# A decoder trunk with product-key experts: VectorE makes the low halves of all V blocks

## The chip, the core and the metric

The kernel runs on one core of a Trainium2 chip. The metric is the device time of one execution in microseconds, from three runs of the kernel before. TensorE does the matmuls, VectorE, ScalarE and GpSimd the elementwise work, and SyncE (SP) issues all the transfers. In profiles they are called PE (PEld for its weight loads), DVE, ACT, POOL and SP.

## What is computed

Two decoder layers on 256 tokens of width 1024. Each layer mixes the tokens (a state-space part and two kinds of attention) and then adds a retrieval of experts. The change concerns the last one, which is cut here to its core:

```python
def peer_ffn(h, wq, k1, k2, u, v):   # u, v: 16384 x 1024
    q = (xc @ wq).reshape(PEER_CHUNK, PEER_HEADS, 2, PEER_HALF)
    ...
    # per token and head: 16 experts e and gates g = softmax(sc)
    u_sel = u[e]
    v_sel = v[e]
    pre = jnp.einsum("td,thkd->thk", xc, u_sel)
    act = jax.nn.gelu(pre, approximate=False) * g
    return jnp.einsum("thk,thkd->td", act, v_sel)
```

Beside this, each layer scales, shifts and gates its inputs by rows that come from a conditioning vector: `mod = silu(c) @ ada_w[l] + ada_b[l]`.

## The kernel before

The kernel gathers nothing: it computes every expert for every token and gives most of them a gate of zero. The 16384 experts are 128 blocks of 128. In the **U stage** each block of `uT` is multiplied with the 256 normed tokens, and a GELU follows; the gates are multiplied in. In the **V stage** each block's activations (128 experts by 256 tokens) are multiplied with the block of `vT` (128 experts by 1024 columns), and all 128 blocks are summed in four PSUM banks, `pacc` (two halves of the tokens by two halves of the columns).

All matmuls are to be near fp32 precision. So every operand is split into a high half, its rounding to fp32r, and a low half, the rest, and a product is made of three matmuls (`mm3`, lines 166 to 168): high by high, high by low, low by high. For a block of V the steps are these:

- `fetch` (L145 to 149): SP issues one transfer of 512 KB into `raw`, a ring of five buffers.
- `split` (L151 to 163): ScalarE rounds it to the high half `wH` (L159); VectorE or GpSimd subtracts for the low half `wL` (L162). Both have rings of three buffers. The argument `low` chooses the engine: "v" is VectorE, anything else GpSimd.
- `v_parts` (L875 to 887): ScalarE rounds the activations to `aH` (L879), VectorE makes `aL` (L880), then comes `split`.
- twelve matmuls of 512 columns: two by two banks, three products each.

The engine of the low half of V block n is set at line 892: GpSimd for n = 0, 3, 6 and so on, 43 of 128 blocks, VectorE for the other 85. In the U stage line 847 and the default of line 684 choose it. They stay.

In layer 0 the V stage carries more: 56 **modulation steps** (`ada_ahead`, L186 to 205) that compute the conditioning rows of the layer's last gate and of layer 1. A step is a transfer of 512 KB into `adaw` (L196), a ring of four, and on VectorE a product with the conditioning row that sums along the way (L178); every second step also adds the bias to two columns (L181). `spread` (L855) hands them out over the blocks in the order in which the code is written.

The order of the instructions on each engine is fixed when the kernel is built. A scheduler walks the program with its own estimate of each duration and issues what it takes to be ready, so VectorE's modulation steps and the transfers on SP are drawn ahead of where `spread` puts them when it holds VectorE to be free. On the chip every engine works through its list in order. Also drawn ahead into layer 0's V stage is GpSimd's work for the masks of layer 1's attention (L335 to 344), and the row of gates that TensorE spreads over the partitions (`gate_row`, L277) and the conditioning row itself (`cond_row`, L127).

```python
        low = lambda n: "g" if n % 3 == 0 else "v"
        for n in range(NKEY - LAST):
            mm = v_parts(n, low(n))
            for c in range(NC):
                for h in range(2):
                    mm(c, h)
            spread(pend, min(1.0, (n + 1) / (NKEY - 8)), len(todo))
```

Of the kernel before, what the change touches and what calls it, by code (L numbers as in the profile page):

```python
# [82 lines left out]
def trunk(ctx: ExitStack, tc: tile.TileContext, x_in, c_in, ada, cols, rows, w_in, w_out, wq, keysT, uT, vT, fg, out, dbg=None):  # L83
# [589 lines left out]
    def peer(l, steps):  # L673
# [215 lines left out]
        h_pool[0].close()  # L889
        todo = steps(es.enter_context(tc.tile_pool(name=f"cond{l}", bufs=1, reuse_waits="tile", side="right")))  # L890
        pend = list(enumerate(todo))
        low = lambda n: "g" if n % 3 == 0 else "v"
        for n in range(NKEY - LAST):
            mm = v_parts(n, low(n))
            for c in range(NC):
# [21 lines left out]
    for l in range(DEPTH):  # L917
# [20 lines left out]
        def steps(pool):  # L938
# [6 lines left out]
            return ada_ahead(jobs, pool)  # L945

        acc = peer(l, steps)
        xs = ExitStack()
        xp = xs.enter_context(tc.tile_pool(name=f"x{l + 1}", bufs=1, reuse_waits="tile"))
# [90 lines left out]
```

## Time and profile before

| | |
|---|---|
| median of three runs | 1995.51 us (1990.01 to 1998.99) |
| the profiled execution: its own time | 1995.14 us |
| its span in the trace | 1993.4 us |
| TensorE matmuls, busy | 1883.4 us (94%) |
| VectorE, busy | 1440.0 us (72%) |
| ScalarE, busy | 966.0 us (48%) |
| GpSimd, busy | 776.0 us (39%) |
| moved by transfers | 376.50 MB, 189 GB/s on average |

Busy shares are averages over stages of different kinds. Matmuls are pipelined: one begins before the one ahead of it has ended, so the pace is read from the starts. The same holds for short VectorE instructions, whose durations overlap a little. An idle time in brackets stands before its instruction, with what ended it.

### The profile page before, as it was taken

The numbers are of one execution on the slowest core, as the hardware profiler recorded it, in microseconds if no ns is written. First come the engines' busy times: TensorE is split into PE (matmuls) and PEld (weight loads), VectorE is DVE, ScalarE is ACT, GpSimd is POOL, SyncE is SP. The second block draws the span as 40 slices with busy tenths as digits, with TensorE's granted clock in tenths as the row PEclk, the third lists the DMA queues.
The fourth block names the chain that finished last, engine by engine and source line by source line (L and its number), as shares of the span: only waits on it lengthen the run. The fifth ranks groups of instructions, "written<-read, shape, count | busy, mean of one in ns | idle before, by whom it ended". The sixth has DMA issues, their size and how long they took to land.

```text
span 1993.4 us, 33885 instructions
## 1 busy us (share of the span) xinstructions
PE 1883.4 (94%) x12864; PEld 1717.4 (86%) x12864; DVE 1440.0 (72%) x2746; ACT 966.0 (48%) x1502; POOL 776.0 (39%) x441
## 2 busy tenths in 40 slices
PE   4898998999999998999989989989999999999998
PEld 3787998999999786788877889979999998888886
DVE  6975999889963998855554669998899435555555
ACT  3564544454444444454545544445444444555444
POOL 5775787000024234322246657960000342222333
PEclk9898999999999999999989989989999999999999
DMA  8863554444455998855634334544444555665653
GB/s 285 281 208 124 164 181 165 134 162 155 160 168 177 348 350 311 295 196 193 194 121 138 127 130 149 189 150 155 155 160 159 177 181 190 206 215 192 195 194 116
DMA packets 103559, 376.50 MB, mean 189 GB/s; under 512 B 12002, under 2 KB 12258, under 8 KB 102756
## 3 DMA queue, kind: packets, MB, share of 16 engines
q1 hardware_dynamic: 103396, 374.34, 55.7%
q8 instruction: 100, 1.64, 0.3%
q14 instruction: 63, 0.52, 0.1%
HBM read 371.15 MB, written 3.15 MB: 188 GB/s over the span
## 4 chain that ended last, share of the span: by engine, by line
PE 69%; DVE 21%; POOL 3%; issue 2%; ACT 2%; DMA 2%; SPq 0%; POOLq 0%; ACTq 0%; DVEq 0%
PE pacc L167 11%; PE pacc L168 10%; PE pacc L166 10%; PE pu L166 9%; PE pu L168 9%; PE pu L167 9%; POOL wL L162 2%; PE pa L167 1%; DVE eq L765 1%; PE pa L168 1%; PE pa L166 1%; DVE eq L764 1%; DVE raw L178 1%; DVE fi L766 1%; DVE a L760 1%
## 5 line engine op out<-in xcount | busy, mean ns | idle before, releaser
L162 POOL TENSOR_TENSOR wL<-raw,wH 128x1024 fp32r<-128x1024 f32 (+2 forms) x364 | 719.8, 1992 | 1142.9 <-ACT wH L159 1134.3
L159 ACT CAST wH<-raw 128x1024 fp32r<-128x1024 f32 (+1 forms) x602 | 628.5, 1045 | 517.7 <-PE pu L167 345.2
L166 PE MATMUL pu<-hH,wH 128*128 128x256 f32 x2048 | 581.5, 284 | 4.8 <-ACT wH L159 2.8
L168 PE MATMUL pu<-hH,wL 128*128 128x256 f32 x2048 | 576.2, 281 | 3.8 <-POOL wL L162 3.8
L167 PE MATMUL pu<-hL,wH 128*128 128x256 f32 x2048 | 575.0, 281 | 0.0
L162 DVE TENSOR_TENSOR wL<-raw,wH 128x1024 fp32r<-128x1024 f32 x324 | 399.3, 1233 | 130.9 <-ACT wH L159 130.8
L167 PE MATMUL pacc<-wL,aH 128*128 128x512 f32 x1024 | 401.4, 392 | 11.6 <-POOL wL L162 8.7
L168 PE MATMUL pacc<-wH,aL 128*128 128x512 f32 x1024 | 399.3, 390 | 0.0
L166 PEld LDWEIGHTS pu<-hH,wH 128*128 128x128 f32 x2048 | 387.5, 189 | 5.3 <-ACT wH L159 3.0
L168 PEld LDWEIGHTS pu<-hH,wL 128*128 128x128 f32 x2048 | 388.0, 189 | 4.3 <-POOL wL L162 4.3
L167 PEld LDWEIGHTS pu<-hL,wH 128*128 128x128 f32 x2048 | 388.1, 189 | 0.0
L880 DVE TENSOR_TENSOR aL<-act,aH 128x256 fp32r<-128x256 f32 x256 | 164.1, 642 | 224.2 <-ACT aH L879 223.7
L166 PE MATMUL pacc<-wH,aH 128*128 128x512 f32 x1024 | 277.7, 389 | 1.2 <-ACT wH L159 1.2
L879 ACT CAST aH<-act 128x256 fp32r<-128x256 f32 x256 | 103.9, 407 | 357.0 <-PE pacc L167 354.7
L167 PEld LDWEIGHTS pacc<-wL,aH 128*128 128x128 f32 x1024 | 192.8, 188 | 57.4 <-POOL wL L162 11.7
L166 PEld LDWEIGHTS pacc<-wH,aH 128*128 128x128 f32 x1024 | 191.9, 188 | 41.4 <-ACT wH L159 1.6
L168 PEld LDWEIGHTS pacc<-wH,aL 128*128 128x128 f32 x1024 | 192.8, 188 | 39.6
L166 PE MATMUL pa<-hH,wH 128*128 128x256 f32 x256 | 75.4, 308 | 13.8 <-ACT hH L260 10.9
L167 PE MATMUL pa<-hL,wH 128*128 128x256 f32 x256 | 76.8, 303 | 1.8 <-DVE hL L261 1.8
L168 PE MATMUL pa<-hH,wL 128*128 128x256 f32 x256 | 76.3, 301 | 1.5 <-POOL wL L162 1.5
L178 DVE SCALAR_TENSOR_TENSOR adaw<-adaw,crow 128x1024 f32<-128x1024 f32 x56 | 70.0, 1259 | 1.2 <-ACT crow L130 1.2
L841 DVE SCALAR_TENSOR_TENSOR act<-pc,act 128x160 f32<-128x160 f32 (+30 forms) x126 | 38.4, 305 | 41.2 <-PE pc L835 40.7
(428 smaller groups left out, 2498.6 us busy)
## 6 DMA issues: line engine op xcount, KB each, us to landing
raw<-in_uT_dram SPq DMA_DIRECT2D x256, 512.0 KB, 3.5
raw<-in_vT_dram SPq DMA_DIRECT2D x256, 512.0 KB, 4.2
adaw<-in_ada_dram SPq DMA_DIRECT2D x56, 512.0 KB, 6.1
raw<-in_ada_dram SPq DMA_DIRECT2D x40, 512.0 KB, 4.5
raw<-in_w_in_dram SPq DMA_DIRECT2D x38, 512.0 KB, 4.1
raw<-in_wq_dram SPq DMA_DIRECT2D x32, 512.0 KB, 3.5
raw<-in_w_out_dram SPq DMA_DIRECT2D x16, 512.0 KB, 3.5
raw<-in_w_in_dram SPq DMA_DIRECT2D x8, 392.0 KB, 3.9
```

The lines of the kernel that those rows point to most:

```text
L159: A.copy(h[:, :n], src)
L162: eng.tensor_tensor(out=lo[:, o:o + step], in0=src[:, o:o + step], in1=h[:, o:o + step].bitcast(F32), op=ALU.subtract)
L166: T.matmul(o, l[0], r[0], start=start, stop=False)
L167: T.matmul(o, l[0], r[1], start=False, stop=False)
L168: T.matmul(o, l[1], r[0], start=False, stop=stop)
L178: V.scalar_tensor_tensor(out=src, in0=src, scalar=1.0, in1=cond, op0=ALU.mult, op1=ALU.mult, accum_out=modc[:, m, k:k + 1])
L760: V.scalar_tensor_tensor(out=a0, in0=a0, scalar=-8.0, in1=ci, op0=ALU.mult, op1=ALU.add)
L764: V.tensor_tensor(out=eq, in0=wide(fab)[:, :, :, None].to_broadcast([P, 2 * NC, TK, TK]), in1=iotar[:, None].to_broadcast([P, 2 * NC, TK, ...
L765: V.tensor_tensor(out=eq, in0=eq, in1=wide(fii)[:, :, None, :].to_broadcast([P, 2 * NC, TK, TK]), op=ALU.mult)
L841: V.scalar_tensor_tensor(out=a, in0=pv[:, lo:hi, :], scalar=1.0 / WSCALE, in1=a, op0=ALU.mult, op1=ALU.mult)
L879: A.copy(aH, act)
L880: V.tensor_tensor(out=aL, in0=act, in1=aH.bitcast(F32), op=ALU.subtract)
```

## The change

One line: the choice of the engine in the V stage no longer depends on the block.

```diff
         h_pool[0].close()
         todo = steps(es.enter_context(tc.tile_pool(name=f"cond{l}", bufs=1, reuse_waits="tile", side="right")))
         pend = list(enumerate(todo))
-        low = lambda n: "g" if n % 3 == 0 else "v"
+        low = lambda n: "v"
         for n in range(NKEY - LAST):
             mm = v_parts(n, low(n))
```

The scheduler places the rest anew. On GpSimd, from the end of layer 0's U stage to the first work of layer 1 (rows of 128x1024 are subtractions of the U and V stages, those of 128x512 belong to layer 1's projections), before:

```order
L162 TENSOR_TENSOR wL<-raw,wH 128x512 x32
L162 TENSOR_TENSOR wL<-raw,wH 128x1024 x51
L123 MEMSET ones 1x128
L162 TENSOR_TENSOR wL<-raw,wH 128x1024 x15
L335 MEMSET mle 128x128
L337 MEMSET mgt 128x128
...
L343 AFFINE_SELECT mask_s<-mask_s 128x128 x2
L344 AFFINE_SELECT mask_s<-mask_s 128x128
L162 TENSOR_TENSOR wL<-raw,wH 128x1024 x30
L162 TENSOR_TENSOR wL<-raw,wH 128x512 x2
```

and of the change:

```order
L162 TENSOR_TENSOR wL<-raw,wH 128x512 x32
L162 TENSOR_TENSOR wL<-raw,wH 128x1024 x51
L123 MEMSET ones 1x128
L162 TENSOR_TENSOR wL<-raw,wH 128x1024 x2
L335 MEMSET mle 128x128
L337 MEMSET mgt 128x128
...
L343 AFFINE_SELECT mask_s<-mask_s 128x128 x2
L344 AFFINE_SELECT mask_s<-mask_s 128x128
L162 TENSOR_TENSOR wL<-raw,wH 128x512 x2
```

The 30 subtractions that stood behind the masks are gone, and 13 of those ahead of them: 96 of this shape become 53.

On VectorE, in the middle of the modulation steps of layer 0's V stage, the same four blocks before (the number behind a name is that of the buffer's tile; the block between `wL_8242` and `wL_8290` is one of GpSimd's):

```order
L162 TENSOR_TENSOR wL_8220<-raw_8217,wH_8219 128x1024
L178 SCALAR_TENSOR_TENSOR adaw_8374,modc_7894<-adaw_8374,crow_7884 128x1024
L880 TENSOR_TENSOR aL_8236<-act1_1742,aH_8235 128x256
L162 TENSOR_TENSOR wL_8242<-raw_8239,wH_8241 128x1024
L178 SCALAR_TENSOR_TENSOR adaw_8422,modc_7894<-adaw_8422,crow_7884 128x1024
L880 TENSOR_TENSOR aL_8258<-act1_1742,aH_8257 128x256
L181 TENSOR_TENSOR modc_7894<-modc_7894,colt_7895 128x2
L880 TENSOR_TENSOR aL_8284<-act1_1742,aH_8283 128x256
L178 SCALAR_TENSOR_TENSOR adaw_8469,modc_7894<-adaw_8469,crow_7884 128x1024
L162 TENSOR_TENSOR wL_8290<-raw_8287,wH_8289 128x1024
```

and of the change:

```order
L162 TENSOR_TENSOR wL_8220<-raw_8217,wH_8219 128x1024
L178 SCALAR_TENSOR_TENSOR adaw_8374,modc_7894<-adaw_8374,crow_7884 128x1024
L181 TENSOR_TENSOR modc_7894<-modc_7894,colt_7895 128x2
L880 TENSOR_TENSOR aL_8236<-act1_1742,aH_8235 128x256
L162 TENSOR_TENSOR wL_8242<-raw_8239,wH_8241 128x1024
L178 SCALAR_TENSOR_TENSOR adaw_8422,modc_7894<-adaw_8422,crow_7884 128x1024
L880 TENSOR_TENSOR aL_8258<-act1_1742,aH_8257 128x256
L162 TENSOR_TENSOR wL_8264<-raw_8261,wH_8263 128x1024
L181 TENSOR_TENSOR modc_7894<-modc_7894,colt_7895 128x2
L880 TENSOR_TENSOR aL_8284<-act1_1742,aH_8283 128x256
L178 SCALAR_TENSOR_TENSOR adaw_8469,modc_7894<-adaw_8469,crow_7884 128x1024
L162 TENSOR_TENSOR wL_8290<-raw_8287,wH_8289 128x1024
```

The subtraction `wL_8264` has come between; the modulation steps keep their places beside the blocks.

On SP, the end of the modulation loads in layer 0's V stage, before:

```order
L148 DMA raw<-in_vT_dram 128x1024
L196 DMA adaw<-in_ada_dram 128x1024
L148 DMA raw<-in_vT_dram 128x1024 x2
L196 DMA adaw<-in_ada_dram 128x1024
L148 DMA raw<-in_vT_dram 128x1024 x64
L148 DMA raw<-in_w_in_dram 128x1024 x6
```

and of the change:

```order
L148 DMA raw<-in_vT_dram 128x1024
L196 DMA adaw<-in_ada_dram 128x1024
L148 DMA raw<-in_vT_dram 128x1024
L196 DMA adaw<-in_ada_dram 128x1024
L148 DMA raw<-in_vT_dram 128x1024 x61
L148 DMA raw<-in_w_in_dram 128x1024 x6
```

The 56 modulation loads now reach three blocks further. In both orders six V loads stand ahead of the first of them, so 58 V loads lay between the first and the last modulation load, and 61 lie there now.

## Rows read from the trace of the kernel before

**Rows 1.** The page's chain that ended last: share of the span by engine.
```profile
PE 69%; DVE 21%; POOL 3%; issue 2%; ACT 2%; DMA 2%; SPq 0%; POOLq 0%; ACTq 0%; DVEq 0%
```

**Rows 2.** Timeline of TensorE: start us, us, engine line op, operands, count [idle before <-releaser].
```profile
647.34 0.85 PE L166 MATMUL pacc<-wH,aH 128*128 128x512 f32 x3
...
653.80 1.12 PE L127 MATMUL pb<-crow,ones 1*128 1x512 f32 x2
655.71 0.50 PE L167 MATMUL pacc<-wL,aH 128*128 128x512 f32 x1
...
666.73 1.05 PE L277 MATMUL pc<-ident,modc 128*128 128x128 f32 x8
...
767.99 0.80 PE L167 MATMUL pacc<-wL,aH 128*128 128x512 f32 x1 [5.30 <-POOL wL L162]
...
1017.55 0.39 PE L168 MATMUL pacc<-wH,aL 128*128 128x512 f32 x1
...
1634.87 0.85 PE L166 MATMUL pacc<-wH,aH 128*128 128x512 f32 x3
...
1983.81 0.39 PE L168 MATMUL pacc<-wH,aL 128*128 128x512 f32 x1
```

**Rows 3.** Stretches: from:to, us, busy us of PE, PEld, DVE, ACT, POOL; PEclk, DMA share, GB/s.
```profile
647.00:1018.00 371.00, 358.11 (x1561) 290.76 (x1559) 270.74 (x356) 177.50 (x263) 120.05 (x55) 1.00 0.76 265
1634.80:1984.30 349.50, 349.40 (x1546) 289.07 (x1545) 182.53 (x217) 173.98 (x258) 102.97 (x44) 1.00 0.58 189
656.00:666.00 10.00, 10.00 (x45) 8.25 (x45) 9.44 (x15) 4.82 (x9) 3.17 (x1) 1.00 1.02 403
...
690.00:760.00 70.00, 67.10 (x292) 54.14 (x291) 69.86 (x98) 32.87 (x49) 22.27 (x14) 1.00 0.97 344
...
746.00:756.00 10.00, 9.88 (x44) 7.88 (x43) 9.96 (x17) 3.30 (x6) 2.45 (x1) 1.00 1.00 363
...
766.00:776.00 10.00, 8.01 (x29) 6.51 (x30) 5.10 (x4) 2.72 (x4) 4.22 (x2) 0.83 0.91 331
```

**Rows 4.** Waits of TensorE, 647 to 1018: who <- whom: us, times, longest us.
```profile
PE pacc L167 <- POOL wL L162: 8.7, 6, 5.3
PE pacc L167 <- DVE wL L162: 2.8, 2, 1.6
PE pacc L166 <- ACT wH L159: 1.2, 1, 1.2
```

**Rows 5.** Timeline of VectorE in layer 0's V stage.
```profile
738.20 0.16 DVE L181 TENSOR_TENSOR modc<-modc,colt 128x2 f32<-128x2 f32 x1
738.28 1.23 DVE L162 TENSOR_TENSOR wL<-raw,wH 128x1024 fp32r<-128x1024 f32 x1
739.42 0.42 DVE L880 TENSOR_TENSOR aL<-act,aH 128x256 fp32r<-128x256 f32 x1
739.75 1.22 DVE L178 SCALAR_TENSOR_TENSOR adaw<-adaw,crow 128x1024 f32<-128x1024 f32 x1
...
740.90 0.42 DVE L880 TENSOR_TENSOR aL<-act,aH 128x256 fp32r<-128x256 f32 x1
...
751.50 2.62 DVE L880 TENSOR_TENSOR aL<-act,aH 128x256 fp32r<-128x256 f32 x1
```

**Rows 6.** Timeline of GpSimd beside the last row of group 5.
```profile
751.40 2.45 POOL L162 TENSOR_TENSOR wL<-raw,wH 128x1024 fp32r<-128x1024 f32 x1 [6.68 <-ACT wH L159]
```

**Rows 7.** Timeline of GpSimd: the first mask instruction and the low half after them.
```profile
758.36 0.21 POOL L335 MEMSET mle<- 128x128 f32 x1 [4.51 <-DVE aL L880]
...
764.64 3.30 POOL L162 TENSOR_TENSOR wL<-raw,wH 128x1024 fp32r<-128x1024 f32 x1
```

**Rows 8.** Timeline of VectorE in layer 1's V stage.
```profile
1709.73 0.43 DVE L880 TENSOR_TENSOR aL<-act,aH 128x256 fp32r<-128x256 f32 x1 [0.54 <-ACT aH L879]
1710.68 1.23 DVE L162 TENSOR_TENSOR wL<-raw,wH 128x1024 fp32r<-128x1024 f32 x1 [0.53 <-ACT wH L159]
```

## The prediction

> **What bounds the kernel now.** I read the chain of waits first: TensorE holds 69% of it, mostly in the matmuls of the U and V stages, and VectorE 21% [rows 1]. So an edit counts only where TensorE is short of an operand. The change touches the V stage of either layer, so next I read the two stages against each other. In the timeline, the V matmuls of layer 0 run from 647.34 to 1017.55 + 0.39 = 1017.94, which is 370.6 us; those of layer 1 run from 1634.87 to 1984.20, which is 349.3 us [rows 2]. Both hold the same 1536 V matmuls, but layer 0 also does 56 modulation steps on VectorE (one 512 KB transfer, one product with a sum, L178). The stretches say why they differ: in layer 1 TensorE is busy for 349.40 of 349.50 us, in layer 0 for 358.11 of 371 [rows 3]. Of the 21.3 us of difference, four small matmuls of layer 0 (L127) take 655.71 - 653.80 = 1.9 us, and eight further gate matmuls (L277; layer 0 has two groups of eight, layer 1 one) at most 1.05 us [rows 2]. The other **18.3 us** are interruptions. Layer 1's 349.3 us over 128 blocks, 2.73 us each, is the pace that matmul issue itself sets.
>
> The waits of TensorE in layer 0's V stage are three: 8.7 us for a low half made by GpSimd (5.3 us of it in one piece), 2.8 us for one made by VectorE, 1.2 us for a high half [rows 4]. That is 12.7 us. The rest of the 18.3 us is what each stop costs when matmuls fill the pipe again, and the lower clock after the long stop: the granted clock was 0.83 in 766 to 776, so part of it ran at the 1.2 GHz level, against 1.00 (2.4 GHz) in the stretches before [rows 3].
>
> Then I looked for what makes these halves late. VectorE was busy for 69.86 of 70 us from 690 to 760 [rows 3]. Part of that is not work: a subtraction aL takes 0.42 us, and the next instruction starts 0.33 us after it (739.42 to 739.75); but the one at 751.50 took 2.62 us. It began 0.10 us after a GpSimd subtraction of 2.45 us and ended 0.27 us after that one's end [rows 5, 6]. So while GpSimd subtracts, VectorE's subtraction stands still. The 5.3 us stop has another origin: GpSimd's mask work for the next layer began only at 758.36, after a wait of 4.51 us for VectorE, and the next low half started behind it in GpSimd's queue at 764.64 and ran until 767.94 [rows 7]; TensorE resumed at 767.99 [rows 2].
>
> **The change part by part.** *GpSimd loses 43 subtractions per layer* (of 96 of this shape in layer 0, 53 are left). Gone with them are all waits of TensorE on GpSimd in this stage, and the collisions with VectorE. The masks stay, but no low half stands behind them. This gives back at most the 18.3 us.
>
> *VectorE gains 43 subtractions per layer*, at 1.14 us each from issue to issue (738.28 to 739.42) [rows 5]: 49 us per layer. In layer 1 a block then needs 1.14 + 0.33 = 1.47 us of VectorE in a pace of 2.73, so the cover is 1.26 us per block and the cost is nothing. In layer 0 the cover is thin. The changed order holds 61 V loads between the first and last modulation load, where there were 58. These 61 blocks ask of VectorE 61 x 1.47 = 89.7 us, and 56 steps at 1.15 us (739.75 to 740.90) plus half a small addition of about 0.2 us each ask 56 x 1.25 = 70 us: together 159.7 us, or 2.62 us per block, against 61 x 2.73 = 166.5 us of TensorE. VectorE stays under the pace by 0.11 us per block. I cost it at nothing; without that cover it is the third rival.
>
> *The transfers* of this stretch are not fewer: 61 + 56 = 117 of 524,288 bytes, 61.3 MB. Bounds come from stretches in which the DMA engines were near full: 403 GB/s (656 to 666) gives 152 us, less than the 166.5; 344 GB/s (690 to 760, share 0.97) gives 178.3, which is 11.8 us over [rows 3]. Between them 363 GB/s (746 to 756, share 1.00) gives 169.0, or 2.5 us over. I take this one, rounded to 3 us, because in it the engines were full, while at 0.97 the queue was partly waiting for buffers that a delayed VectorE released.
>
> The Trainium skill, HBM Reference, section Specifications (TRN2), gives about 425 GB/s for a core that streams alone and about 358 for each of two that share a domain. By the first figure the stretch would take 144 us and nothing would come back; by the second 171.3 us and 4.8 us would come back, for 1981.6 us. The 403 GB/s of the trace is over the shared figure, so the trace speaks for the first; the sum above does without either.
>
> *The queues that are passed.* On SP the V and modulation loads interleave in nearly the same alternation, now one to one; the load of x moves behind a few of them, and is needed only after the stage. On GpSimd the work of the next layer comes up earlier, with nobody waiting. In layer 1 TensorE has no wait in the V stage, so nothing can be gained there.
>
> **Sum.** 1995.14 us is the profiled execution's own time (0.4 us under the median of 1995.51). 1995.14 - 18.3 = 1976.8; plus 3 us for transfers: **1980 us**.
>
> **Rivals.**
> 1. *Transfers bound layer 0's stretch.* Once VectorE no longer holds back the loads, the DMA engines set the pace at the 344 GB/s of 690 to 760. For it: share 0.97 there. Against it: 10 us at 363 and at 403 GB/s. It returns 11.8 us: 1976.8 + 11.8 = 1988.6 us, within 0.5% of before.
> 2. *Many short stops take the place of few long ones.* VectorE at 2.62 of 2.73 us is in order: a low half stands behind a modulation step, and TensorE waits briefly. For it: the 2.8 us that TensorE already waits for VectorE's halves [rows 4]. Against it: those are two stops only, in a stretch where VectorE was full and was losing time to collisions. If every second of 61 blocks costs 0.5 us, 15 us return: 1992 us.
> 3. *VectorE becomes the bound of the stretch, and the kernel is slower.* In layer 1 VectorE stands still twice per block for ScalarE, 0.54 and 0.53 us (from 1709.73 to 1710.68) [rows 8]. If these waits stay in layer 0's stretch, because the fixed order leaves no modulation step to fill them, a block takes 2.62 + 1.07 = 3.69 us, 0.96 over the pace, and 61 blocks cost 58.6 us: 1976.8 + 58.6 = 2035 us. It decides from 0.42 us of waiting per block (0.11 are free, and 61 x 0.31 eats up the 18.7 us to the median); from 0.58 us it is over 0.5% slower. Against it: from 690 to 760, with about one step per block as after the change, VectorE waited for 0.14 us in all. For it: the margin of 4% has never been run.
>
> That the change does nothing can be left out: the order on GpSimd shows the subtractions gone.
>
> **How the numbers follow.** The forecast has 0.60, the first rival 0.17, the second 0.12, the third 0.11. A measurement of this kernel can tell about 0.5%, 10 us, from no change (its three runs spread over 9 us), so faster means under 1985.5 us and slower over 2005.5. The forecast is on the faster side, rivals 1 and 2 are within, the third is slower: 0.60, 0.29, 0.11. The range begins at 1974, the 1976.8 with nothing returned and 3 us for the spread of runs; it reaches over both rivals within to 1997, and leaves out the third rival and a rest.
>
> **What would show it.** Right: layer 0's V stage lasts 352 to 357 us instead of 370.6, layer 1's stays at 349; the mean of aL falls to about 0.42 us in both layers; TensorE has no wait on GpSimd there, and under 4 us on VectorE's halves; the granted clock stays 1.00 in layer 0's V stage. Rival 1 would show as a DMA share of 0.97 or more with high halves late; rival 2 as many stops under 1 us on VectorE's low halves; rival 3 as VectorE with idle time before wL and aL in layer 0 while TensorE waits for them. Wrong altogether: stops that stay with aL at 0.42 us, or a changed time outside the V stages.

## The result and the profile after

The changed kernel takes 1977.97 us (median of four executions, 1976.86 to 1979.84), the one before 1996.11 us (median of four). The ratio is 0.9911, with a 95% interval of 0.9898 to 0.9924: 18 us less. The forecast was 1980 us with a range of 1974 to 1997, and a chance of 0.60 for faster.

The profiled execution took 1976.86 us, its span is 1975.2 us. The timeline of TensorE in the same two stages, first and last V matmul of either layer, answers to [rows 2]:

```profile
649.28 0.39 PE L166 MATMUL pacc<-wH,aH 128*128 128x512 f32 x1
...
1001.27 0.39 PE L168 MATMUL pacc<-wH,aL 128*128 128x512 f32 x1
...
1616.51 0.39 PE L166 MATMUL pacc<-wH,aH 128*128 128x512 f32 x1
...
1965.53 0.39 PE L168 MATMUL pacc<-wH,aL 128*128 128x512 f32 x1
```

Layer 0's V stage lasts 1001.66 - 649.28 = 352.4 us, where it was 370.6; layer 1's lasts 1965.92 - 1616.51 = 349.4 us, where it was 349.3. The difference of 18.2 us equals that of the spans, 1993.4 - 1975.2. In part this is luck: layer 0's V stage also begins 1.9 us later, and from its end to layer 1's V stage 614.9 us pass instead of 616.9. The two cancel. Neither is shown to come from the change: between the V stages, where the code is the same, 614.8 to 617.9 us pass in the kernels of the second to fifth experiments. The view of stretches, with the columns of [rows 3], shows TensorE without a gap:

```profile
648.00:1002.00 354.00, 353.66 (x1569) 291.85 (x1567) 272.72 (x401) 178.04 (x263) 10.75 (x13) 1.00 0.78 278
1616.00:1966.00 350.00, 349.92 (x1550) 289.60 (x1548) 212.12 (x260) 174.10 (x258) 1.87 (x2) 1.00 0.57 189
656.00:766.00 110.00, 110.00 (x490) 90.37 (x490) 103.23 (x170) 56.45 (x84) 7.76 (x11) 1.00 0.99 376
```

The three waits of [rows 4] have no successor: in neither V stage does TensorE wait for anything now. The page's groups for VectorE and GpSimd read:

```profile
L162 POOL TENSOR_TENSOR wL<-raw,wH 128x512 fp32r<-128x512 f32 (+2 forms) x278 | 502.6, 1827 | 885.9 <-ACT wH L159 879.1
L162 DVE TENSOR_TENSOR wL<-raw,wH 128x1024 fp32r<-128x1024 f32 x410 | 502.4, 1225 | 206.7 <-ACT wH L159 206.3
...
L880 DVE TENSOR_TENSOR aL<-act,aH 128x256 fp32r<-128x256 f32 x256 | 108.3, 424 | 107.4 <-ACT aH L879 107.1
```

In the whole kernel VectorE makes 410 low halves in one piece each, and GpSimd 278 pieces; the mean of aL is 0.424 us, as that of an undisturbed one in [rows 5]. GpSimd still does the mask work late, but its next instruction comes only at 997.39, so no low half of the V stage stands behind it:

```profile
754.87 0.21 POOL L335 MEMSET mle<- 128x128 f32 x1 [110.46 <-DVE aL L880]
```

### The profile page after: what moved, and what is told of

Same layout as the page of the kernel before. It is cut to its first block, busy times and chain, and to the rows that moved or that the text cites. A ratio compares the mean times of both kernels' runs of the same rounds, so it can differ in the third digit from the quotient of the medians.

```text
span 1975.2 us, 33891 instructions
## 1 busy us (share of the span) xinstructions
PE 1876.7 (95%) x12864; PEld 1715.1 (87%) x12864; DVE 1471.2 (74%) x2832; ACT 966.3 (49%) x1502; POOL 561.5 (28%) x355
## 4 chain that ended last, share of the span: by engine, by line
PE 73%; DVE 20%; POOL 2%; DMA 2%; ACT 2%; issue 1%; SPq 0%; POOLq 0%; ACTq 0%; DVEq 0%
PE pacc L167 12%; PE pacc L168 12%; PE pacc L166 12%; PE pu L166 9%; PE pu L168 9%; PE pu L167 9%; PE pa L167 1%; PE pa L168 1%; DVE eq L765 1%; PE pa L166 1%; DVE eq L764 1%; POOL wL L162 1%; DMA raw<-in_ada_dram 1%; DVE fi L766 1%; DVE raw L178 1%
## 5 line engine op out<-in xcount | busy, mean ns | idle before, releaser
L162 POOL TENSOR_TENSOR wL<-raw,wH 128x512 fp32r<-128x512 f32 (+2 forms) x278 | 502.6, 1827 | 885.9 <-ACT wH L159 879.1
L162 DVE TENSOR_TENSOR wL<-raw,wH 128x1024 fp32r<-128x1024 f32 x410 | 502.4, 1225 | 206.7 <-ACT wH L159 206.3
L880 DVE TENSOR_TENSOR aL<-act,aH 128x256 fp32r<-128x256 f32 x256 | 108.3, 424 | 107.4 <-ACT aH L879 107.1
```

What stands on the lines that cost most here:

```text
L162: eng.tensor_tensor(out=lo[:, o:o + step], in0=src[:, o:o + step], in1=h[:, o:o + step].bitcast(F32), op=ALU.subtract)
L880: V.tensor_tensor(out=aL, in0=act, in1=aH.bitcast(F32), op=ALU.subtract)
```

## The experiments

Ratios are those of each kernel to the kernel before, run beside it. The changed kernel's 0.9911 is the mark to compare with.

**1. The queue behind the masks alone.** The kernel before, with one more block on VectorE.

```diff
-        low = lambda n: "g" if n % 3 == 0 else "v"
+        low = lambda n: "g" if n % 3 == 0 and not (l == 0 and n == 39) else "v"
```

> The kernel before, with one low half moved: that of V block 39 of layer 0, the one that stands behind the mask work in GpSimd's queue, goes to VectorE. Theory 1 (the single stop of 5.30 us is the queue behind the masks): that stop goes with its restart and its stretch at the lower clock, and with them about 7 us: 1989 us; the short stops stay. Theory 2 (collisions on VectorE cause all of it, and the stop would come at the next block anyway): under 2 us, 1994 to 1996 us.

Measured: 1987.78 us, ratio 0.9953 (0.9939 to 0.9966), about 9 us less. The waits of TensorE in layer 0's V stage:

```profile
PE pacc L167 <- POOL wL L162: 4.0, 6, 1.0
PE pacc L167 <- DVE wL L162: 2.8, 2, 1.6
PE pacc L166 <- ACT wH L159: 1.2, 1, 1.2
```

The stop of 5.30 us is gone: the longest wait on GpSimd is 1.0 us, one short stop has come in its place, and the other two rows stand as before. The first and last V matmul of layer 0:

```profile
649.55 0.86 PE L166 MATMUL pacc<-wH,aH 128*128 128x512 f32 x3
...
1014.12 0.39 PE L168 MATMUL pacc<-wH,aL 128*128 128x512 f32 x1
```

The stage is 365.0 us long, 5.6 less than before. So theory 1 holds: the long stop was a queue. By the medians the one block was worth half of the gain, within the stage 5.6 of 18.2 us, under a third. The spans differ by 7.3 us: the V stage begins 2.2 us later, and 3.8 us less pass from it to layer 1's, where the edit changes no line. Only the 5.6 us are shown to be the block's.

**2. The change in one layer at a time.**

```diff
-        low = lambda n: "g" if n % 3 == 0 else "v"
+        low = lambda n: "g" if n % 3 == 0 and l == 1 else "v"
```

> The change in layer 0 alone; layer 1 keeps GpSimd's low halves. Theory of the prediction (all of the gain lies in layer 0, where TensorE stops): 1978 us, within 2 us of the changed kernel. Rival (layer 1's collisions cost something too): 1980 to 1990 us.

The other kernel has `l == 0` in its place.

> The change in layer 1 alone. Theory of the prediction: nothing is gained, 1996 us within 3 us. Rival: some of the 18 us appears here.

Measured: 1978.62 us, ratio 0.9909 (0.9893 to 0.9924), in layer 0 alone; 1997.81 us, ratio 1.0004 (0.9995 to 1.0013), in layer 1 alone. Both are as the prediction's theory expects: all of the gain is in layer 0. In layer 1 VectorE was held in the same way, as the mean of aL there shows (0.605 us before, from 1634.8 to 1984.3), but TensorE never waited for it.

```profile
L880 DVE TENSOR_TENSOR aL<-act,aH 128x256 fp32r<-128x256 f32 x125 | 75.6, 605 | 141.9 <-ACT aH L879 141.8
```

**3. GpSimd busy as before, but with nothing to deliver.** The changed kernel, with reads on GpSimd that serve nobody.

```diff
             h, lo = split(fetch(vT[l, i // 2, :, i % 2 * D:(i % 2 + 1) * D]), low)
+            if i % 3 == 0:
+                junk = fp.tile([P, 1024], F32, tag="junk", name="junk", bufs=1)
+                G.tensor_tensor(out=junk, in0=h.bitcast(F32), in1=h.bitcast(F32), op=ALU.subtract)
```

> The changed kernel with, for every third V block, an added subtraction on GpSimd that reads the block's high half twice and writes a tile that nobody reads: GpSimd is as busy as before, but no operand of TensorE comes from it. Theory 1 (GpSimd's reading holds VectorE): about 20 of them lie in layer 0's stretch of 61 blocks and cost VectorE up to 2.2 us each, 44 us against a slack of 7: the stretch grows by up to 37 us, 1990 to 2015 us, with aL at a mean of 0.6 us or more, and TensorE waiting for VectorE's halves. Theory 2 (the stops came from halves that a slow GpSimd made late): 1978 us, no stops.

Measured: 1998.83 us, ratio 1.0013 (1.0004 to 1.0022). The whole gain is lost, though no operand of the V stage comes from GpSimd. In the waits of TensorE, then in the timelines of VectorE and GpSimd:

```profile
PE pacc L167 <- DVE wL L162: 14.0, 16, 1.3
```

```profile
700.44 1.21 DVE L162 TENSOR_TENSOR wL<-raw,wH 128x1024 fp32r<-128x1024 f32 x1
...
703.06 2.90 DVE L162 TENSOR_TENSOR wL<-raw,wH 128x1024 fp32r<-128x1024 f32 x1
```

```profile
702.49 2.39 POOL L884 TENSOR_TENSOR junk<-wH 128x1024 f32<-128x1024 f32 x1 [7.62 <-ACT wH L159]
```

A low half that starts within a GpSimd subtraction takes 2.90 us instead of 1.21. These holds of about 1.7 us put VectorE over the pace, and TensorE stops 16 times. Theory 1 holds: 22 reads lie between 648 and 850, and 21 us were lost against up to 37 expected. VectorE also makes all the low halves in this run, so the 21 us don't say what the holds cost in the kernel before.

**4. GpSimd as busy, but only writing.**

```diff
+            if i % 3 == 0:
+                junk = fp.tile([P, 1024], F32, tag="junk", name="junk", bufs=1)
+                tiny = fp.tile([P, 1], F32, tag="tiny", name="tiny", bufs=2)
+                for _ in range(3):
+                    G.memset(junk, 0.0)
+                A.activation(tiny, h[:, 0:1].bitcast(F32), AF.Copy, scale=junk[:, 0:1])
```

> The changed kernel with, for every third V block, three added memsets of 128x1024 on GpSimd into a tile of which ScalarE reads one column, so that they fall beside the block. GpSimd is about as busy as in the run with the added reads, but it only writes. Theory 1 (what holds VectorE is GpSimd's reading): no gain is lost, 1978 us within 3 us, aL at a mean of 0.42 us. Theory 2 (any use of the memory by GpSimd holds VectorE): 1990 to 2000 us, as with the reads.

Measured: 1978.40 us, ratio 0.9903 (0.9887 to 0.9920). Nothing is lost, as theory 1 expects. Groups from 650 to 820:

```profile
L162 DVE TENSOR_TENSOR wL<-raw,wH 128x1024 fp32r<-128x1024 f32 x59 | 72.2, 1223 | 7.0 <-ACT wH L159 6.6
...
L880 DVE TENSOR_TENSOR aL<-act,aH 128x256 fp32r<-128x256 f32 x60 | 25.6, 427 | 7.7 <-ACT aH L879 7.5
```

```profile
L886 POOL MEMSET junk<- 128x1024 f32 x60 | 57.4, 956 | 102.9 <-ACT tiny L887 100.7
```

GpSimd writes for 57.4 us beside it, and the means of wL and aL stay at 1.223 and 0.427 us. So it is not GpSimd's being busy that holds VectorE but its subtractions, which read. The Trainium skill, SBUF — State Buffer, section Who interferes with whom, says the same: a VectorE instruction with two inputs in SBUF contends with a GpSimd instruction that reads SBUF, not with one that only writes. These two runs agree, with 1.7 us and with nothing. That any reading would do is not shown: in the changed kernel GpSimd's AFFINE_SELECT, which reads and writes one tensor, ran from 759.70 to 762.63, and a modulation product beside it took 1.30 us instead of 1.22.

```profile
759.52 1.30 DVE L178 SCALAR_TENSOR_TENSOR adaw<-adaw,crow 128x1024 f32<-128x1024 f32 x1
```

**5. How thin VectorE's cover is.** The changed kernel, with aL made twice.

```diff
             V.tensor_tensor(out=aL, in0=act, in1=aH.bitcast(F32), op=ALU.subtract)
+            junk = fp.tile([P, S], F32, tag="junk", name="junk", bufs=2)
+            V.tensor_tensor(out=junk, in0=act, in1=aH.bitcast(F32), op=ALU.subtract)
```

> The changed kernel with aL made twice, the second time into a tile that nobody reads: 0.33 us more of VectorE per V block. The order then holds 50 V loads among the 56 modulation loads. Theory 1 (the third rival's mechanism: beyond its slack VectorE sets the pace of the stretch): 50 blocks ask of it 50 x 1.80 + 70 = 160 us against 50 x 2.73 = 136.5 us of TensorE, 23 us over: 1978 + 23 = 2001 us less what is made ahead, 1993 to 2001. Theory 2 (blocks made ahead cover it): under 1985 us.

Measured: 1994.58 us, ratio 0.9975 (0.9966 to 0.9985). That is 0.0064 over the changed kernel's ratio, or 13 us, and within theory 1's range. In the stretch VectorE is full:

```profile
690.00:764.00 74.00, 72.86 (x297) 53.62 (x296) 74.00 (x139) 33.27 (x49) 0.00 (x0) 1.00 0.96 352
```

The starts of the first matmuls of consecutive blocks, in TensorE's timeline:

```profile
700.38 1.07 PE L166 MATMUL pacc<-wH,aH 128*128 128x512 f32 x4
...
703.41 1.07 PE L166 MATMUL pacc<-wH,aH 128*128 128x512 f32 x4
...
706.36 1.07 PE L166 MATMUL pacc<-wH,aH 128*128 128x512 f32 x4
...
709.38 1.07 PE L166 MATMUL pacc<-wH,aH 128*128 128x512 f32 x4
```

They are (709.38 - 700.38) / 3 = 3.0 us apart, against a pace of 2.73. TensorE's weight loads, from 690 to 764, wait in nearly every block for VectorE's low half, 9.8 us in all, where it is 0.8 us in the whole of the changed kernel:

```profile
PEld pacc L167 <- DVE wL L162: 9.8, 23, 1.5
```

The stage lasts 366.4 us, 14 over the changed kernel's. This is what the third rival feared, VectorE as the bound, but by another way: 0.33 us more work per block, and not the waits for ScalarE that the rival counted on.

**6. The same idea in another stage.** During the top-k choice GpSimd made the low halves of U blocks and of the query weights. Five kernels move them, all on top of the changed one. First the first 40 U blocks of a layer:

```diff
-        def u_mm(ip, low="gg"):
+        def u_mm(ip, low="vv"):
...
-        def u_pair(ip, dst, low="gg"):
+        def u_pair(ip, dst, low="vv"):
```

> The changed kernel with the low halves of the first 40 U blocks too on VectorE, which lie beside the top-k choice. There small VectorE instructions of 32 elements take about 1 us on average, and TensorE stops at the end of the choice (VectorE is late). Theory 1 (a GpSimd subtraction costs VectorE about 1.7 us by its reads, and 1.14 us if VectorE makes it itself): some 30 of them in the choice, 17 us less on VectorE per layer, and up to 15 us less of TensorE's stop: 1950 to 1970 us. Theory 2 (most instructions of the choice read one operand and were not held): VectorE gets 30 x 1.14 = 34 us more per layer, and the stop grows: 2000 to 2040 us.

Measured: 1972.17 us, ratio 0.9869 (0.9853 to 0.9886). By the ratios that is 8 us less than the changed kernel. The median is 2 us outside theory 1's range; theory 2's slower kernel did not come. Then the query weights alone (`lambda q: "h"` becomes `"v"`):

> The changed kernel with only the low halves of the query weights on VectorE (16 per layer, which GpSimd makes in two pieces each). Theory 1: 16 x 1.14 = 18 us more work and 32 pieces x about 1 us fewer holds per layer: 1965 to 1978 us. Theory 2 (no holds saved): 1990 to 2010 us.

Measured: 1977.38 us, ratio 0.9892 (0.9876 to 0.9909), no difference from the changed kernel that can be told; it lies at the end of theory 1's range. In the run with the U blocks, TensorE has one long wait in this part of each layer. In layer 0:

```profile
245.78 0.58 PE L168 MATMUL pu<-hH,wL 128*128 128x256 f32 x1 [6.58 <-DVE wL L162]
```

Two kernels leave the first pair, or the first two, on GpSimd:

> As the run with the first 40 U blocks on VectorE, but the first pair of them back on GpSimd. In that run TensorE waits once per layer, 6.6 us, for the low half of the first pair, which stands on VectorE behind the choice of a head. Theory 1 (GpSimd is right where VectorE's queue is full and one low half is urgent): both waits go, 1972 - 13 = 1959 us, with 1 or 2 us of holds come back. Theory 2 (the next pair waits in the same way): 1968 to 1973 us.

> As that, with the first two pairs on GpSimd. Theory 1: nothing more to gain, 1959 us, or 1 to 4 us slower by two more subtractions that hold VectorE. Theory 2: the wait goes only now, 1959 against 1968 to 1973 us with one pair.

Measured: 1979.04 us (0.9905, 0.9890 to 0.9920) and 1984.45 us (0.9937, 0.9924 to 0.9951). Both are slower than with none, and outside the ranges of both theories; theory 1 fell. The wait only moves to the first low half that VectorE does make, and it grows in layer 0 to 10.0 us with one pair and 14.9 us with two:

```profile
256.66 0.58 PE L168 MATMUL pu<-hH,wL 128*128 128x256 f32 x1 [10.02 <-DVE wL L162]
```

```profile
267.60 0.58 PE L168 MATMUL pu<-hH,wL 128*128 128x256 f32 x1 [14.94 <-DVE wL L162]
```

So the next kernel takes GpSimd out of the choice altogether, the U blocks and the query weights both:

> The run with the first 40 U blocks on VectorE, and the query weights' low halves there too, so that GpSimd reads nothing while the choice runs. Theory 1 (TensorE's wait of 6.6 us per layer for the first U block comes from VectorE being behind its place in the order, which knows nothing of the holds by GpSimd's query halves): without holds the wait goes, 1972 - 13 = 1959 us, to 1966. Theory 2 (VectorE is behind because the choice and the added halves are too much work): 1972 to 1990 us, with a longer wait.

Measured: **1953.89 us, ratio 0.9790 (0.9776 to 0.9803)**, the fastest of all, 5 us below theory 1's range. The V stages are as in the changed kernel (352.4 and 349.4 us); layer 0's begins 11.9 us sooner, and 11.2 us less pass from it to layer 1's. From 200 to 660 TensorE's long wait for a low half is gone:

```profile
PE pu L168 <- DVE wL L162: 0.3, 1, 0.3
```

Groups of VectorE from 204 to 352 in the changed kernel, then in this one:

```profile
L765 DVE TENSOR_TENSOR eq<-eq,fii 128x1024 f16<-128x1024 f16 x8 | 13.3, 1660 | 0.0
...
L760 DVE SCALAR_TENSOR_TENSOR a<-a,ci 128x32 f32<-128x32 f32 x8 | 9.3, 1168 | 0.0
...
L754 DVE TENSOR_SCALAR a<-r 128x32 f32<-128x32 uint32 x8 | 7.6, 950 | 0.0
...
L710 DVE MAX8 vv<-sc 128x8 f32<-128x128 f32 x30 | 6.8, 273 | 0.0
```

```profile
L162 DVE TENSOR_TENSOR wL<-raw,wH 128x1024 fp32r<-128x1024 f32 x49 | 59.8, 1222 | 2.8 <-ACT wH L159 2.8
...
L710 DVE MAX8 vv<-sc 128x8 f32<-128x128 f32 x32 | 7.7, 286 | 0.0
...
L765 DVE TENSOR_TENSOR eq<-eq,fii 128x1024 f16<-128x1024 f16 x8 | 5.6, 694 | 0.0
...
L760 DVE SCALAR_TENSOR_TENSOR a<-a,ci 128x32 f32<-128x32 f32 x8 | 1.5, 187 | 0.0
...
L754 DVE TENSOR_SCALAR a<-r 128x32 f32<-128x32 uint32 x8 | 1.4, 181 | 0.0
```

Instructions of 32 elements fall from about 1 us to 0.18. VectorE makes 49 low halves more (59.8 us) in a stretch of 148 us in which it was full before. Neither step alone does it: by the ratios 8 us and nothing that can be told, against 24 together. With GpSimd still reading, VectorE was behind its place in the order, and the first urgent half waited; with 11 low halves more in the stretch (49, where the run with the U blocks has 38) it does not. So it was not too much work that made it late. The holds that are gone remain as the cause, though the order was also placed anew.

**7. One step too far.** The same, with the mixers' low halves on VectorE as well (`LOWPAT = "v"`).

> As the run before, with the low halves of the mixers' weights on VectorE too (GpSimd made them in two pieces). Theory 1 (moving GpSimd's reads pays wherever VectorE is loaded): 1940 to 1950 us. Theory 2 (it pays only where holds delay what TensorE waits for; in the mixers TensorE waits for VectorE's chains of small dependent steps, and VectorE gets more in front of them): 1954 to 1975 us.

Measured: 1961.82 us, ratio 0.9818 (0.9805 to 0.9831), slower than without by 8 us in the medians and 6 by the ratios. It is a loss in layer 0 and a gain in layer 1: layer 0's V stage begins 11.8 us later, and 4.4 us less pass from it to layer 1's. TensorE's longest wait is now for GpSimd:

```profile
PE pc L555 <- POOL segr L553: 17.1, 1, 17.1
```

This product of the state-space part had itself waited for VectorE. Timelines of VectorE and GpSimd:

```profile
101.29 0.17 DVE L542 SCALAR_TENSOR_TENSOR a<-dt,ah 128x16 f32<-128x16 f32 x1
```

```profile
101.61 1.88 POOL L553 TENSOR_TENSOR segr<-mle,a 128x512 f32<-128x512 f32 x1 [1.84 <-DVE a L542]
```

In the run before, VectorE makes this `a` at 82.82. So theory 2 holds in layer 0, and in its reason: VectorE comes 18 us later to a small step on which TensorE waits.

## Why the prediction was right

- *What bounds the kernel.* The 18.3 us of interruptions in layer 0's V stage were the gain: the stage lost 18.2 us, and TensorE's three waits are gone. The reading by which layer 1 has nothing to give is shown by the run that changes it alone (ratio 1.0004).
- *Two causes of late halves.* The queue behind the masks is shown by moving one block (9 us by the medians, 5.6 within the stage), and the holds of VectorE by adding reads (21 us back, without any late GpSimd half). The runs don't divide the rest of the 18.2 us between the holds and the slow GpSimd subtraction by itself.
- *VectorE's thin cover.* 2.62 us of work in 2.73 us held: VectorE was busy for 103.23 of 110 us from 656 to 766, and TensorE did not wait. With 0.33 us more per block it did.
- *Transfers.* This term was mis-sized: 3 us were to come back and nothing did. Layer 0's stage is 3.0 us longer than layer 1's, no more than the small matmuls at up to 2.95 us. The DMA engines moved 376 GB/s from 656 to 766, where 363 had been taken; the 344 GB/s of [rows 3] was no limit of theirs, since the same stretch of program now runs faster. Without the 3 us the sum is 1976.8, and the median lies 1.2 us over it, which is within the spread of its four executions.
- *Rivals.* Of the first rival's signs only the DMA share came (0.99), with no high half late; the second left no trace. The third did not come in: from 656 to 766 VectorE stood still for ScalarE for 5.8 us in all, before wL and aL, or 0.14 us in each of 40 blocks, where the rival had 1.07. That VectorE can become the bound with little more work is shown by the fifth experiment. The groups of VectorE in that stretch of the changed kernel:

```profile
L162 DVE TENSOR_TENSOR wL<-raw,wH 128x1024 fp32r<-128x1024 f32 x39 | 47.7, 1224 | 3.4 <-ACT wH L159 3.2
...
L880 DVE TENSOR_TENSOR aL<-act,aH 128x256 fp32r<-128x256 f32 x39 | 16.5, 424 | 2.6 <-ACT aH L879 2.6
```

## What to carry to other kernels

In this kernel a subtraction moved to GpSimd was not taken off VectorE: to make it takes VectorE 1.14 us, and when GpSimd made it and the two met, VectorE lost about 1.7 us. Look for short VectorE instructions with long means beside a busy GpSimd, and move the reads away together: beside the choice, one half of them gained 8 us, the other nothing that can be told, and both together 24. Before that, see who waits: the same holds cost nothing in layer 1, where TensorE never waited for VectorE.

## What the runs showed of the hardware

- The hold works the other way as well. With aL made twice VectorE issues two-operand instructions without a gap, and GpSimd's mask work, which took 6.3 us in the kernel before (758.36 to 764.64 in [rows 7]), took from 767.27 to 809.15. Timeline of GpSimd in that run:

```profile
767.27 0.21 POOL L335 MEMSET mle<- 128x128 f32 x1 [122.37 <-DVE junk L882]
...
768.29 5.55 POOL L336 TENSOR_SCALAR_AFFINE_SELECT mle<-mle 128x128 f32<-128x128 f32 x1
...
803.03 6.12 POOL L344 TENSOR_SCALAR_AFFINE_SELECT mask_s<-mask_s 128x128 f32<-128x128 f32 x1
```

- Not only VectorE's two-operand instructions are held: TENSOR_SCALAR on one tensor of 32 elements fell from 0.950 to 0.181 us, while MAX8, also on one tensor, stood at 0.273 and 0.286 us. In the changed kernel one of the former, here with the GpSimd subtraction beside it, ends 0.04 us after that one:

```profile
233.28 1.59 DVE L754 TENSOR_SCALAR a<-r 128x32 f32<-128x32 uint32 x1
```

```profile
232.43 2.40 POOL L162 TENSOR_TENSOR wL<-raw,wH 128x1024 fp32r<-128x1024 f32 x1 [0.26 <-ACT wH L159]
```

- The DMA engines were not at their limit at a share of 0.97 and 344 GB/s: the changed kernel has 376 GB/s over 110 us at a share of 0.99.
